# A softmax over long rows: the last six chunks' stores issued by SyncE behind the last load instead of by ScalarE

## The chip, the cores and the metric

The kernel runs on one core of a Trainium2 chip. The metric is the device time of one execution in microseconds (us), the median of several runs. The core's compute engines used here are VectorE (DVE) and ScalarE (ACT); SyncE (SP) computes nothing and issues transfers. Transfers between the device memory and the core's on-chip memory are carried out by 16 DMA engines; an instruction on SP or ACT only starts one. All transfers started by SP stand in one queue, in the profile q1, all those started by ACT in another, q10.

## What is computed

A softmax over the last axis of a tensor of 16 x 256 rows with 32768 float32 elements each, with a temperature of 1.0:

```python
def setup_inputs():
    batch, seq, vocab = 16, 256, 32768
    return {
        "logits": np.random.randn(batch, seq, vocab).astype(np.float32),
        "temperature": 1.0,
    }

def reference(logits, temperature):
    scaled = logits / temperature
    scaled = scaled - scaled.max(axis=-1, keepdims=True)
    exp_scaled = np.exp(scaled)
    return (exp_scaled / exp_scaled.sum(axis=-1, keepdims=True)).astype(np.float32)
```

The input is 537 MB and the output as much. Each is moved once.

## The kernel before

**Tiling.** Each row of 32768 elements is cut into two halves of 16384, which lie in two neighbouring partitions. So 64 rows fill the 128 partitions and form a group `g`; there are `G` = 64 groups. A group is worked on in `C` = 2 chunks of `_CW` = 8192 columns: 128 partitions x 8192 float32, which is 32 KB in each partition and 4.19 MB in all. The chunks are numbered `i` = 0 to 127 over the whole run (`n_chunks` = 128); group 63 has chunks 126 and 127.

**Buffers.** Six chunk buffers (`_BUFS` = 6) lie side by side in the tensor `X`; chunk `i` uses buffer `i % 6`. A chunk is loaded into its buffer, changed in place, and stored from it. So load `i + 6` can be issued only when store `i` has landed.

**One group** (`compute`, called once for each group). For each chunk DVE takes the negated maximum of its 8192 columns (line 156, output `t`), and ACT takes the exponential in place with that maximum as bias, and sums it up on the way (line 170). When both chunks are done, DVE swaps the values of neighbouring partitions (line 183), so that both halves of a row know each other's maximum and sum; the common maximum (line 187), the correction factors of the chunks (line 194, on ACT, output `ee`), the row's sum (line 200) and its reciprocal (line 212) follow. All of these are tiny. Then DVE scales each chunk in place by its factor and the reciprocal (line 221). Only after that can a chunk be stored.

**Edges.** In the last group (`g == G - 1`) the step is `_EDGE` = 4096 columns and no longer 8192: chunks 126 and 127 are loaded, reduced, scaled and stored in two halves of 2.10 MB each. The first group is loaded in halves as well.

**Order by hand.** Each engine's instructions are executed in the order in which the program issues them; the order between engines is made by semaphores. A `Stream` (`sp`, `dve`, `act`) stands for an engine: its `wait` makes that engine wait for given semaphore values, and its `done` counts an instruction of that engine. A `Landing` counts a buffer's transfers that have arrived. `load(i)` (lines 103 to 118) is issued by SP, with a wait for the store that used the buffer before (line 106), and the transfer itself on line 112. `store(i)` (lines 120 to 133) is issued by ACT, with a wait for DVE's scaling of the piece (line 126, `scaled[i, s]`), and the transfer on line 128. The main loop (lines 232 to 241) first issues six loads, and then for each group: `compute(g)`, and for each of its chunks `store(i)` and `load(i + 6)`, as long as there is such a chunk. So the last load, that of chunk 127, is issued in the round of chunk 121, and no load stands behind it in the program. At the end SP waits for all stores (line 242; the wait itself is on line 31, in `Stream.wait`).

Of the kernel before, what the change touches and what calls it, by code (L numbers as in the profile page):

```python
# [8 lines left out]
_CW = 8192  # L9
_BUFS = 6  # L10
_EDGE = 4096


class Stream:
# [41 lines left out]
def kernel(  # L56
# [6 lines left out]
    nc = tc.nc  # L63
# [15 lines left out]
    n_chunks = G * C  # L79
# [10 lines left out]
    sp = Stream(nc, nc.sync, "sp")  # L90
    dve = Stream(nc, nc.vector, "dve")
    act = Stream(nc, nc.scalar, "act")
    loads = [[Landing(nc, f"ld{b}{h}") for h in range(_CW // _EDGE)] for b in range(_BUFS)]
    stores = [Landing(nc, f"st{b}") for b in range(_BUFS)]
    scaled = {}
# [4 lines left out]
    def spans(total, step):  # L100
        return [(s, min(step, total - s)) for s in range(0, total, step)]
# [18 lines left out]
    def store(i):  # L120

        g, c = divmod(i, C)
        b = i % _BUFS
        rows = slice(g * P, (g + 1) * P)
        for s, n in spans(_CW, _EDGE if g == G - 1 else _CW):
            act.wait(scaled[i, s])
            stores[b].add(
                nc.scalar.dma_start(
                    out=o[rows, c * _CW + s : c * _CW + s + n],
                    in_=X[:, b * _CW + s : b * _CW + s + n],  # L130
                )
            )
        freed[b] = [stores[b].token()]
# [100 lines left out]
    for g in range(G):  # L234
        compute(g)
        for c in range(C):
            i = g * C + c
            store(i)
            j = i + _BUFS
            if j < n_chunks:  # L240
                load(j)
# [36 lines left out]
```

## Time and profile before

| What | Value |
|---|---|
| Time, median of 3 runs | 2497.72 us (2497.65 to 2498.47) |
| Time of the profiled execution | 2497.72 us |
| Its span, first to last instruction | 2495.9 us |
| DVE busy | 1723.7 us, 69% of the span |
| ACT busy | 944.5 us, 38% of the span |
| Moved | 1073.84 MB, mean 430 GB/s |
| q1 (loads, issued by SP) | 536.88 MB, 49.9% of the 16 DMA engines' span |
| q10 (stores, issued by ACT) | 536.88 MB, 49.8% of the 16 DMA engines' span |
| Load of a whole chunk, issue to landing | 26.6 us (median) |
| Store of a whole chunk, issue to landing | 49.4 us (median) |
| Maximum of a whole chunk, DVE line 156 | 8.69 us |
| Exponential of a whole chunk, ACT line 170 | 7.12 us |

The page gives busy times by engine, the span in 40 slices, the queues, the chain of work that ended last, the costliest groups of instructions, and the transfers. Such a page is read beside closer views of the same trace: the chain in order of time, the instructions in order of time, who waited for whom, and the engines' busy time and the transfers' rate in chosen stretches. Times in these views are in us from the start of the span. The DMA share in a short stretch can come out slightly over 1.

"SPq" and "ACTq" are the sequencers of SP and ACT, in which transfers are issued; "L112" is line 112.

### The profile page before, as it was taken

What the parts mean: (1) busy time and instruction counts of PE and PEld (TensorE: products, weight loads), DVE (VectorE), ACT (ScalarE), POOL (GpSimd) and SP (SyncE); (2) the same over time, 40 slices, a digit from 0 to 9 for tenths busy, and PEclk for the clock granted to TensorE, in tenths of its full rate; (3) what the DMA queues carried; (4) which work ended last, traced back from release to release, by engine and by line L of the source; (5) the groups of instructions that cost most, each with busy time, mean ns of one, the idle gap of its engine ahead of it and who ended that gap; (6) DMA issues with size and microseconds to landing.
All of it is one profiled execution on the core that took longest, in us unless ns stands there. A gap on an engine that the chain in (4) does not pass through costs nothing.

```text
span 2495.9 us, 1288 instructions
## 1 busy us (share of the span) xinstructions
DVE 1723.7 (69%) x644; ACT 944.5 (38%) x325; POOL 0.2 (0%) x4
## 2 busy tenths in 40 slices
DVE  6777766767667676676766767767667676676763
ACT  3344334343343433434334333343333433434332
POOL 0000000000000000000000000000000000000000
DMA  9999999999999999999999999999999999999997
GB/s 412 432 433 435 430 436 430 436 430 436 432 434 435 431 435 430 436 431 434 435 431 436 429 437 430 436 432 433 435 430 435 431 436 432 434 434 431 435 433 337
DMA packets 37738, 1073.84 MB, mean 430 GB/s; under 512 B 4192, under 2 KB 4192, under 8 KB 4192
## 3 DMA queue, kind: packets, MB, share of 16 engines
q1 hardware_dynamic: 19008, 536.88, 49.9%
q10 hardware_dynamic: 18720, 536.88, 49.8%
q14 instruction: 10, 0.08, 0.0%
HBM read 536.87 MB, written 536.87 MB: 430 GB/s over the span
## 4 chain that ended last, share of the span: by engine, by line
DMA 62%; another core or an unknown queue 15%; DVE 15%; ACT 7%; SPq 0%; issue 0%; DVEq 0%
DMA out_dram<-xs 38%; DMA xs<-in_logits_dram 23%; DVE t L156 9%; ACT xs L170 7%; DVE xs L221 5%; SPq L112 0%; ACT ee L194 0%; DVE row L212 0%; DVE row L187 0%; DVE t L183 0%; DVE junk L200 0%; DVE row L200 0%; SPq L273 0%; DVEq L31 0%
## 5 line engine op out<-in xcount | busy, mean ns | idle before, releaser
L170 ACT ACTIVATE xs<-xs,t 128x8192 f32<-128x8192 f32 (+1 forms) x130 | 912.1, 7016 | 1498.5 <-DVE t L156 1498.5
L156 DVE TENSOR_REDUCE t<-xs 128x1 f32<-128x8192 f32 (+1 forms) x130 | 1111.1, 8551 | 263.8 <-DMA xs<-in_logits_dram 263.8
L221 DVE TENSOR_SCALAR xs<-xs,ee,row 128x8192 f32<-128x8192 f32 (+1 forms) x130 | 576.6, 4478 | 2.3
L183 DVE LOAD_MASK_SELECT t<-t x64 | 0.9, 14 | 463.1 <-ACT xs L170 463.1
L194 ACT ACTIVATE ee<-t,row 128x4 f32<-128x4 f32 x64 | 19.0, 297 | 27.0 <-DVE row L187 27.0
L200 DVE CUSTOM_DVE_ANT_1 junk<-ee,t 128x4 f32<-128x4 f32 x64 | 10.4, 163 | 23.3 <-ACT ee L194 23.3
L170 ACT ACTIVATION_READ_ACCUMULATOR xs<-xs,t 128x1 f32 x130 | 24.2, 186 | 0.0
L212 DVE RECIPROCAL row<-row 128x1 f32<-128x1 f32 x64 | 10.5, 164 | 2.2
L187 DVE TENSOR_REDUCE row<-t 128x1 f32<-128x4 f32 x64 | 10.1, 157 | 2.2
L183 DVE STREAM_SHUFFLE t<-t 128x4 f32<-128x4 f32 x64 | 9.9, 155 | 0.0
L200 DVE DVE_READ_ACCUMULATOR2_ANT row<- 128x1 f32 x64 | 5.3, 82 | 0.0
L170 ACT ACT_TABLE_LOAD x1 | 1.3, 1283 | 0.9 <-SPq L82 0.9
L259 POOL MEMSET const-bfloat16-1.0<- 128x1 bf16 x1 | 0.1, 101 | 0.0
L259 POOL MEMSET const-uint8-127<- 128x1 uint8 x1 | 0.1, 101 | 0.0
L259 POOL MEMSET const-float32-0.0<- 128x1 f32 x1 | 0.1, 98 | 0.2 <-issue 0.2
L259 POOL MEMSET const-float32-1.0<- 128x1 f32 x1 | 0.1, 98 | 0.0
## 6 DMA issues: line engine op xcount, KB each, us to landing
out_dram<-xs ACTq DMA_DIRECT2D x126, 4096.0 KB, 49.4
xs<-in_logits_dram SPq DMA_DIRECT2D x124, 4096.0 KB, 26.6
xs<-in_logits_dram SPq DMA_DIRECT2D x8, 2048.0 KB, 21.2
out_dram<-xs ACTq DMA_DIRECT2D x4, 2048.0 KB, 10.2
```

Of the source, the lines that this page charges most:

```text
L156: nc.vector.tensor_reduce(out=t[:, k : k + 1], in_=xs, axis=mybir.AxisListType.X, op=A.max, negate=True)
L170: nc.scalar.activation(out=xs, in_=xs, func=Exp, bias=t[:, k : k + 1], scale=inv_t, accum_out=t[:, K + k : K + k + 1],)
L183: nc.vector.stream_shuffle(out=t[:, 2 * K : 4 * K], in_=t[:, 0 : 2 * K], mask=swap)
L187: nc.vector.tensor_reduce(out=r[:, 0:1], in_=tv[:, :, 0, :], axis=mybir.AxisListType.XY, op=A.min)
L194: nc.scalar.activation(out=ev, in_=tv[:, :, 0, :], func=Exp, bias=r[:, 0:1], scale=-1.0)
L200: nc.vector.tensor_tensor_reduce(out=j_[:, 0 : 2 * K].rearrange("p (a k) -> p a k", a=2), in0=ev, in1=tv[:, :, 1, :], scale=1.0, scalar=0. ...
L212: rc = dve.done(nc.vector.reciprocal(out=r[:, 2:3], in_=r[:, 1:2]))
L221: nc.vector.tensor_scalar(out=xs, in0=xs, scalar1=e[:, k : k + 1], scalar2=r[:, 2:3], op0=A.mult, op1=A.mult,)
L259: nc = _bacc.Bacc("TRN2", target_bir_lowering=False, num_devices=1)
```

## The change

A constant `_LATE` = 6 is added. For the last six chunks, 122 to 127 (those of groups 61, 62 and 63), the wait for the scaling and the issue of the store go to SP; for all chunks before, they stay with ACT. Sizes, pieces, semaphores and buffers are the same, and so are all loads and the arithmetic.

```diff
 _BUFS = 6
 _EDGE = 4096
+_LATE = 6
...
         rows = slice(g * P, (g + 1) * P)
+        q = sp if i >= n_chunks - _LATE else act
         for s, n in spans(_CW, _EDGE if g == G - 1 else _CW):
-            act.wait(scaled[i, s])
+            q.wait(scaled[i, s])
             stores[b].add(
-                nc.scalar.dma_start(
+                q.engine.dma_start(
                     out=o[rows, c * _CW + s : c * _CW + s + n],
                     in_=X[:, b * _CW + s : b * _CW + s + n],
                 )
             )
```

In program order, the eight issues of these stores (four of a whole chunk, four of half a chunk) stand on SP behind the load of chunk 127 and ahead of the last wait.

## The prediction

> **What bounds the kernel now.** I read the profile in this order: the page's slices, its chain, the same chain near the end, the engines there, and the transfers stretch by stretch. First the slices, and the share of the span by engine in the chain that ended last:
>
> ```profile
> DMA  9999999999999999999999999999999999999997
> GB/s 412 432 433 435 430 436 430 436 430 436 432 434 435 431 435 430 436 431 434 435 431 436 429 437 430 436 432 433 435 430 435 431 436 432 434 434 431 435 433 337
> ...
> DMA 62%; another core or an unknown queue 15%; DVE 15%; ACT 7%; SPq 0%; issue 0%; DVEq 0%
> ```
>
> The transfer engines are full in every slice but the last, at about 433 GB/s, loads and stores together. The kernel must move 1073.8 MB and the rate doesn't change, so time can be won only where the transfers stand idle: at the start, and in the last slice, which moves 337. The table by stretch (columns: us, busy time of DVE, ACT and POOL, clock, DMA share, GB/s) shows where in that slice:
>
> ```profile
> 5.00:45.00 40.00, 22.85 (x10) 14.72 (x5) 0.00 (x0) 1.00 1.01 433
> ...
> 2442.00:2458.00 16.00, 4.42 (x1) 3.80 (x2) 0.00 (x0) 1.00 1.00 431
> 2458.00:2463.00 5.00, 1.14 (x1) 0.00 (x0) 0.00 (x0) 1.00 0.95 410
> 2463.00:2464.00 1.00, 1.00 (x1) 0.00 (x0) 0.00 (x0) 1.00 0.23 98
> 2464.00:2466.00 2.00, 2.00 (x1) 0.00 (x0) 0.00 (x0) 1.00 0.08 33
> 2466.00:2467.50 1.50, 0.28 (x1) 1.19 (x1) 0.00 (x0) 1.00 0.05 22
> 2467.50:2469.00 1.50, 0.00 (x0) 1.50 (x1) 0.00 (x0) 1.00 0.00 0
> 2469.00:2474.50 5.50, 3.88 (x8) 1.41 (x3) 0.00 (x0) 1.00 0.00 0
> 2474.50:2475.50 1.00, 1.00 (x1) 0.00 (x0) 0.00 (x0) 1.00 1.23 524
> ```
>
> The first row is loads alone: 433 GB/s. At the end the share falls to a quarter at 2463, to 0.05 (less than one of the 16 transfer engines) after 2466, and is nothing from 2467.5 to 2474.5. The packet records say it more exactly: 13 transfer engines end their work near 2463.1, two at 2465.2 and 2465.7, one at 2467.54; the next packet begins at 2474.57. The slowest transfer engine is thus idle for **7.03 us**, and every stretch before that it is busy. Why it is idle, the chain in order of time says:
>
> ```profile
> 2412.33 0.33 SPq L112
> 2412.65 0.04 issue
> 2412.70 49.14 DMA xs<-in_logits_dram
> 2461.83 0.02 issue
> 2461.86 4.43 DVE t L156
> ```
>
> The last half of chunk 127's load is issued at 2412.70 and takes 49.14 us, because stores 122 to 125 run beside it. Its maximum, exponential, row factors and scaling follow with no transfer left to cover them, and the last four stores (line 128) are issued from 2473.73 on.
>
> **The change, part by part.** I number chunks as the code does. *What ACT loses*: eight store issues (chunks 122 to 125 whole, 126 and 127 in halves) of 0.338 us each at line 128, 2.7 us, and the waits on line 126. ACT idles there for 18.1 us at a time for DVE's maxima, so this is worth nothing; without that idle time it would gain 2.7 us of ACT.
>
> *What SP gets*: the same eight waits and issues, behind load 127, its last. Issues on SP took 0.328 us (line 112), 0.926 us in the longest case, so 2.6 to 7.4 us in all; I take 0.33 each, since the first store stands free. Behind them on SP are only the later stores and the end's wait (line 242); no load can be held up. Nobody waits for these eight stores but that last wait, as no load reuses their buffers.
>
> *What is held back*: store 122 is ready at 2386.3 and is issued then, yet lands 40.6 us later, at 2426.9: it stands on ACT's queue behind stores 120 and 121. Store 121 was issued at 2352.0 and lands 60.3 us later, at 2412.3, which is also what releases load 127. So until 2412.3 nothing changes. From there ACT's queue is empty and SP's holds the rest of load 126, load 127, then the stores.
>
> *The loads*: the first half of 126 gets the transfer engines from 2403.3 (load 125 lands: issue 2376.6 plus 26.6) to 2417.8 (2396.0 plus 21.8): 2.10 MB in 14.5 us, 144 GB/s, a third of 433. At 2412.3, 62% of it is there; 0.8 MB and three halves of 2.1 MB are left, 7.1 MB. Alone at 433 GB/s (the 5 to 45 row) they take 16.4 us and land by **2428.7** in place of 2461.8. The other end of this price is the present 144 GB/s beside stores, with which they would land where they do now; I take the first, as nothing runs beside them.
>
> *The arithmetic*, from these two rows of the order in time:
>
> ```profile
> 2420.38 9.00 DVE L221 TENSOR_SCALAR xs<-xs,ee,row 128x8192 f32<-128x8192 f32 x2
> 2429.30 8.74 DVE L156 TENSOR_REDUCE t<-xs 128x1 f32<-128x4096 f32 x2
> ```
>
> DVE is free at 2429.4 and then has all four halves: 4 x 4.37 = 17.5 us, to 2446.9 (ACT's 3.9 us for each keeps up). From the end of the last maximum (2461.86 + 4.43 = 2466.29) to the first store's issue (2473.73) is 7.44 us today, so that store is issued at 2454.3 and the fourth 7.0 us later, at 2461.3.
>
> *The stores*: 122 to 125 are 16.8 MB, 38.8 us at 433 GB/s: 2428.7 + 38.8 = 2467.5, the moment at which they end today, as it must be with the same bytes. By then the last group's stores have long been issued: with 0.84 us from issue to first packet (2473.73 to 2474.57) the first needs to go by 2466.7, and goes 12.4 us earlier. For the transfer engines that end at 2463.1 the margin is 8 us. So the last stores follow without a gap. Today they take from 2474.57 to the last landing, 2480.7 + 14.0 = 2494.7; all of it moves ahead by 7.03.
>
> *Unknown*: no row shows a store behind a load on one queue. Below, the turn costs nothing, as between loads on SP's queue; above, one pause of 0.84 us to start plus 0.34 us for a landing (last packet 2494.40, landed 2494.74), 1.2 us. I take nothing: that is how two transfers follow each other there. Unknown too is whether the lag of the slowest transfer engine stays. Today the gap lets it catch up; if the others could take it over, another 2467.5 - 2463.1 = 4.4 us would be won, and this is the lower bound. I take it as staying: its 32 KB packets take 1.213 us with the others idle and with them busy.
>
> **Sum**: span 2495.9 - 7.0 = 2488.9. This execution took 2497.72 us, 1.8 more than its span, and is the median of the three runs (2497.65 to 2498.47). Forecast 2497.72 - 7.03 = **2490.7 us**, 0.28% less.
>
> [...]
>
> **Rivals.** *The last stores come late*: if the loads of 126 and 127 land more than 12 us after 2428.7, the gap stays in part. For it: their rate today. Against: ACT's queue is empty then. Half of the gap left: 2494.2; all of it: 2497.7. The same 2497.7 holds if SP's stores somehow don't stand behind load 127, but the loop issues it after store 121 and before store 122.
>
> *One queue pauses between transfers* (the slower side): two queues can cover each other's starts, one can't. From 2412.3 SP's queue has eleven transfers to come after the half in progress: three load halves, four whole stores, four half stores. A pause of 1.2 us at each is 13.2 us, less 7.0: 2503.9. It decides from six pauses on. Against: the eight loads at the start stood on that one queue alone, and by issue and time to landing came at 8.3, 13.2, 18.0, 23.0, 32.7 and 42.4 us, 4.9 for a half and 9.7 for a whole chunk, which is 433 GB/s without a pause. For: those are loads behind loads only. A pause at the turn alone gives 2491.9.
>
> *The lag is won too*: 2490.7 - 4.4 = 2486.3. Against: the 22 GB/s of the last transfer engine at 2466, which didn't quicken.
>
> **How the numbers follow.** Forecast 0.80, own range 2489.8 to 2492.0. Lag won 0.05. Late stores or no effect 0.09. Pauses 0.06. Below 2492.7 (0.2%, or 5.0 us, is about what a measurement tells from no change) lie the first two, 0.85; within 0.2%, 0.09; slower, 0.06. The range 2488.0 to 2493.5 holds the forecast, the pause at the turn, and the near parts of the lag and of late stores.
>
> **What would show it.** In the profile after: load 127 lands at about 2428.7, 16 us after its issue and not 49; the stretch 2412 to 2428 has only loads, at 433 GB/s; the maxima of the last group follow each other from 2429.4 with no wait for a load; the last four stores are issued between 2454 and 2462 and the last takes some 26 us to land, not 14; no stretch of zero transfers; the chain ends in stores. I am wrong if the share drops at 2428 or between stores, if the last four are issued later than 2466, or if the stores' rate on SP's queue is below 420 GB/s.

## The result and the profile after

The changed kernel takes **2490.88 us** (median of 8 runs, 2490.03 to 2491.78) against 2497.68 us for the kernel before (8 runs, 2497.07 to 2498.69). The ratio is 0.9972, with a 95% interval of 0.9961 to 0.9983. The profiled execution took 2490.77 us, with a span of 2489.0 us, 6.9 us less than before.

First the page of the kernel after: its slices, and its two transfer queues (packets, MB, share of the 16 DMA engines' span).

```profile
DMA  9999999999999999999999999999999999999999
GB/s 412 430 437 430 436 432 432 436 430 437 430 435 433 431 436 431 436 431 434 433 431 437 430 436 432 432 435 430 437 431 434 433 431 437 430 436 432 432 426 393
...
q1 hardware_dynamic: 20160, 562.05, 52.4%
q10 hardware_dynamic: 17568, 511.71, 47.6%
```

The last slice is full where it was 7 tenths full, and moves 393 GB/s where it moved 337. The last slice but one has 426 against 433; in the slices before, the two lines differ by up to 6 GB/s in both directions. The 25 MB of six chunks' stores have moved from q10 to q1. The stretches at the end, with the same columns as before (us, busy time of DVE, ACT and POOL, clock, DMA share, GB/s):

```profile
2458.00:2463.00 5.00, 3.01 (x2) 0.00 (x0) 0.00 (x0) 1.00 0.97 419
2463.00:2464.00 1.00, 0.00 (x0) 0.00 (x0) 0.00 (x0) 1.00 0.81 344
2464.00:2466.00 2.00, 0.00 (x0) 0.00 (x0) 0.00 (x0) 1.00 1.07 459
...
2469.00:2474.50 5.50, 0.00 (x0) 0.00 (x0) 0.00 (x0) 1.00 1.01 432
2474.50:2482.00 7.50, 0.00 (x0) 0.00 (x0) 0.00 (x0) 1.00 1.01 435
2482.00:2484.00 2.00, 0.00 (x0) 0.00 (x0) 0.00 (x0) 1.00 0.48 205
2484.00:2486.00 2.00, 0.00 (x0) 0.00 (x0) 0.00 (x0) 1.00 0.15 66
2486.00:2487.50 1.50, 0.00 (x0) 0.00 (x0) 0.00 (x0) 1.00 0.05 22
```

Where the kernel before moved nothing for 7 us, this one moves 432 GB/s. DVE has nothing to do any more by 2463: its work lies beside the stores. The slow fall at the end, which stood at 2463 to 2467.5 before, is now the very end: twelve of the 16 transfer engines are done near 2483, the other four follow, the last at 2487.5.

The chain in order of time and the instructions show how the arithmetic moved (start, us, what):

```profile
2403.21 8.70 DVE t L158
...
2420.31 9.00 DVE xs L223 x2
2429.31 17.32 DVE t L158 x4
2446.63 0.02 issue
2446.65 3.81 ACT xs L172 x2
...
2451.63 9.38 DVE xs L223 x4
```

The four maxima of the last group follow the scaling of the group before at once, 17.32 us together. Before, the last two of them waited 8.87 and 10.54 us for their loads. The second half of chunk 127's load is issued at 2412.6 and lands 17.0 us later, not 49.1. The last four stores are issued at 2454.1 to 2461.0 and the last of them lands 26.8 us later, at 2487.8, where the kernel before had 2494.7.

### The profile page after: what moved, and what is told of

It is laid out like the page before. It is cut to its first block, busy times and chain, and to the rows that moved or that the text cites. A ratio compares the mean times of both kernels' runs of the same rounds, so it can differ in the third digit from the quotient of the medians.

```text
span 2489.0 us, 1288 instructions
## 1 busy us (share of the span) xinstructions
DVE 1723.5 (69%) x644; ACT 944.5 (38%) x325; POOL 0.2 (0%) x4
## 4 chain that ended last, share of the span: by engine, by line
DMA 58%; DVE 18%; another core or an unknown queue 15%; ACT 8%; SPq 0%; issue 0%; DVEq 0%
DMA out_dram<-xs 37%; DMA xs<-in_logits_dram 21%; DVE t L158 11%; ACT xs L172 7%; DVE xs L223 6%; ACT ee L196 0%; SPq L113 0%; DVE row L214 0%; DVE row L189 0%; DVE t L185 0%; DVE junk L202 0%; DVE row L202 0%; SPq L275 0%; DVEq L32 0%
## 6 DMA issues: line engine op xcount, KB each, us to landing
out_dram<-xs ACTq DMA_DIRECT2D x122, 4096.0 KB, 49.7
```

## The experiments

Each is compared with the kernel before, run on the same chip beside it; those of one set share these runs. The diffs are against the kernel after.

### How many stores go behind the loads

**Four, three or two chunks in place of six** (runs late4, late3, late2):

```diff
-_LATE = 6
+_LATE = 4
```

> Only chunks 124 to 127 are stored by SP; 122 and 123 stay with ACT. Theory (the gain is the idle time of the slowest transfer engine between store 125's end and the last four stores): loads 126 and 127 keep a third of 433 GB/s until store 123 lands at 2441.4, have 2.9 MB left then, and land at 2441.4 + 6.7 = 2448.1, before 2467.5 - 0.84 - 7.44 - 4.43 = 2454.8. No gap is left: 2490.9 us, as with six. Rival (the gain comes from the stores moved, a share for each): two thirds of 6.8 us, 2493.2 us.

Measured: 2490.7 us (2490.15 to 2490.95), ratio 0.9971 (0.9959 to 0.9982). As with six: two stores fewer behind the loads cost nothing. The packet records of this run have no gap.

> Only chunks 125 to 127 are stored by SP. Theory: load 127 keeps a third of 433 GB/s until store 124 lands at 2456.4, has 0.7 MB left then and lands at 2458.1; the first of the last stores is issued at 2458.1 + 4.43 + 7.44 = 2470.0 and moves its first byte at 2470.8, 2.9 us after the slowest transfer engine ran dry at 2467.9. So 4.1 of 7.0 us are won: 2493.6 us. Rival (a share for each store moved): half of 6.8 us, 2494.3 us, with no gap in sight or the whole gap.

Measured: 2494.66 us (2493.96 to 2495.0), ratio 0.9987 (0.9978 to 0.9996). Its stretches at the end:

```profile
2463.00:2464.00 1.00, 0.55 (x1) 0.41 (x1) 0.00 (x0) 1.00 0.15 66
2464.00:2468.50 4.50, 0.63 (x6) 3.69 (x3) 0.00 (x0) 1.00 0.08 36
2468.50:2471.80 3.30, 3.26 (x3) 0.00 (x0) 0.00 (x0) 1.00 0.00 0
2471.80:2474.50 2.70, 2.70 (x2) 0.00 (x0) 0.00 (x0) 1.00 1.15 485
```

The gap is there in part: from the last packet of store 125 (2468.46) to the next packet (2471.84) it is 3.4 us, against 7.03 before. The time itself is nearer to the rival's 2494.3 than to the 2493.6 worked out; it is the part of a gap, which the rival doesn't have, that tells the two apart. Of the miss of 1.1 us, 0.3 is in the working: it counts its 2.9 us from the landing of store 125 (2467.87) and not from its last packet (2467.54). The rest lies ahead of the gap: load 127 lands at 2459.1, 1.0 us later than worked out, and store 125 0.9 us later than before. Why was not taken apart; in late2, whose stores 122 to 125 run beside the loads as before, its last packet comes just as late.

> Only chunks 126 and 127 are stored by SP. Theory: the stores 122 to 125 run beside the last loads as before, load 127 lands at 2461.8, and the whole gap of 7 us stays: 2497.7 us. Rival (a share for each store moved): a third of 6.8 us, 2495.4 us. A third theory, that the last four stores go faster from SP's queue than from ACT's, says less than 2497 us as well.

Measured: 2498.31 us (2497.5 to 2498.88), ratio 1.0001 (0.9992 to 1.0009): no change. The gap is 7.03 us as before (packets end at 2468.46, the next begins at 2475.49), and the last four stores take 6.3 to 14.0 us to land, as before. So SP's queue is not the faster one for them, and the gain is no share for each store moved: with 2, 3, 4 and 6 chunks it is nothing, 3.2, 7.1 and 6.8 us. It goes by how much of the gap is closed.

### The same order without SP

**All stores by ACT, but 122 to 125 held back until load 127 has landed** (run held_act). ACT issues them between the exponentials of groups 62 and 63:

```diff
-        q = sp if i >= n_chunks - _LATE else act
+        q = act
+        if n_chunks - _LATE <= i < n_chunks - 2:
+            act.wait(*landed[n_chunks - 1])
...
-            store(i)
+            if i < n_chunks - _LATE:
+                store(i)
...
+        if g == G - 2:
+            for i in range(n_chunks - _LATE, n_chunks - 2):
+                store(i)
+        if g == G - 1:
+            for i in range(n_chunks - 2, n_chunks):
+                store(i)
```

> All stores stay with ACT; those of chunks 122 to 125 are issued by ACT between the exponentials of groups 62 and 63, each after a wait for load 127's landing. Theory (what counts is that the last loads go first, so that the last group's arithmetic lies beside stores; by which engine they are issued counts for nothing): loads land at 2429, the stores follow after a pause of 0.84 to 2.3 us, the last ones without a gap: 2491.5 to 2493 us. Rival (the gain is SP's queue itself, or ACT relieved of eight issues): 2497.7 us as before, or more, since ACT now waits.

Measured: 2492.3 us (2491.81 to 2493.34), ratio 0.9978 (0.9968 to 0.9987). Four fifths of the gain, 5.5 of 6.8 us, come without a single store on SP; it is the order that counts. What is missing is a pause, which the stretches of this run show:

```profile
2412.00:2424.00 12.00, 4.39 (x7) 7.40 (x3) 0.00 (x0) 1.00 0.99 423
2424.00:2428.70 4.70, 4.70 (x2) 0.00 (x0) 0.00 (x0) 1.00 0.11 45
2428.70:2430.00 1.30, 1.30 (x2) 0.00 (x0) 0.00 (x0) 1.00 0.95 403
```

From 2424.0 to 2428.7 most transfer engines have no work while the last ones finish the loads; only after the landing at 2428.7 do the stores start. Store 122 lands 11.9 us after load 127, where 9.7 us is the time of a chunk: the pause costs the slowest transfer engine 2.2 us. Queued behind the loads on one queue, the stores start without it, but there the turn from loads to stores costs 0.8 us, as the section on the prediction shows. The difference, 1.4 us, is that of the two times, 2492.3 and 2490.9.

### How much arithmetic the stores cover

**Two or four idle maxima on DVE in the last group** (runs extra2 and extra4; the result isn't used):

```diff
+_EXTRA = 2
...
+    Z = nc.alloc_sbuf_tensor("extra", [P, 8], fp32)
...
         dve.wait(sums[-1])
+        if g == G - 1:
+            for k in range(_EXTRA):
+                dve.done(
+                    nc.vector.tensor_reduce(
+                        out=Z[:, k : k + 1], in_=xs, axis=mybir.AxisListType.X, op=A.max, negate=True
+                    )
+                )
```

> The kernel after with two more maxima of 4096 columns on DVE in the last group, behind its last exponential (their result is not used): 8.7 us more between the last load and the last four stores. Theory: the first of these stores is issued at 2454.1 + 8.7 = 2462.8 and has its first packet at 2463.6, before the slowest transfer engine runs dry at 2468.0: nothing is lost, 2490.9 us. Rival (the arithmetic of the last group still stands on the path to the end): 2490.9 + 8.7 = 2499.6 us.

Measured: 2490.62 us (2490.36 to 2491.15), ratio 0.9971 (0.9959 to 0.9982). The added work is there, in the instructions of this run in order of time, and costs nothing:

```profile
2450.81 8.74 DVE L190 TENSOR_REDUCE extra<-xs 128x1 f32<-128x4096 f32 x2 [3.87 <-ACT xs L175]
```

> The same with four more maxima, 17.4 us. Theory: the first of the last stores is issued at 2471.5, first packet at 2472.3, 4.3 us after the slowest transfer engine runs dry at 2468.0: a gap opens again, 2490.9 + 4.3 to 4.7 = 2495.4 us. Rival (arithmetic on the path): 2490.9 + 17.4 = 2508.3 us. A theory in which the cover is as wide as the whole of the stores 122 to 125: 2490.9 us.

Measured: 2495.45 us (2495.22 to 2495.86), ratio 0.999 (0.9981 to 0.9999). The stretches of this run:

```profile
2463.00:2464.00 1.00, 1.00 (x2) 0.00 (x0) 0.00 (x0) 1.00 0.23 98
2464.00:2467.70 3.70, 3.70 (x3) 0.00 (x0) 0.00 (x0) 1.00 0.08 35
2467.70:2472.00 4.30, 3.83 (x8) 0.30 (x1) 0.00 (x0) 1.00 0.00 0
2472.00:2474.50 2.50, 2.50 (x2) 0.00 (x0) 0.00 (x0) 1.00 0.99 419
```

17.4 us of added work cost 4.6 us, and the gap accounts for it: by the packet records it is 4.5 us (2467.55 to 2472.07). So the room in the kernel after is between 8.7 and 17.4 us, and by this cost 17.4 - 4.6 = 12.8 us.

### Two more stores on SP

**Eight chunks** (run late8). Now the stores of 120 and 121, for whose landing loads 126 and 127 wait, stand on SP's queue among these loads:

```diff
-_LATE = 6
+_LATE = 8
```

> Chunks 120 to 127 are stored by SP, so that the stores of 120 and 121 stand on SP's queue between its last loads, and loads 126 and 127 are issued only when they have landed. Theory: nothing is queued elsewhere by then, and the transfer engines pause twice for a landing and a start, 0.34 + 0.84 us each: 2490.9 + 2.4 = 2493.3 us, with two short dips of the DMA share near 2400 and 2420. Rival (more stores on SP's queue is better, a share for each): 2490.9 - 2.3 = 2488.6 us. Rival (one queue pauses between all its transfers): far more than 2.4 us.

Measured: 2499.96 us (2499.37 to 2500.26), ratio 1.0008 (0.9999 to 1.0016). The two further stores throw away the whole gain; the 2.1 us above the kernel before are not clear of noise. The theory had the sign and missed the size: 9.1 us over the kernel after, not 2.4. The stretches of this run show two kinds of loss:

```profile
2385.00:2391.00 6.00, 6.00 (x3) 0.00 (x0) 0.00 (x0) 1.00 0.95 300
2391.00:2399.00 8.00, 8.00 (x1) 0.00 (x0) 0.00 (x0) 1.00 1.00 430
2399.00:2402.00 3.00, 3.00 (x2) 2.47 (x1) 0.00 (x0) 1.00 0.05 22
2402.00:2403.50 1.50, 1.50 (x1) 1.50 (x1) 0.00 (x0) 1.00 0.20 44
2403.50:2407.00 3.50, 3.50 (x1) 3.24 (x2) 0.00 (x0) 1.00 0.93 360
2407.00:2411.00 4.00, 1.09 (x1) 2.88 (x1) 0.00 (x0) 1.00 1.06 455
2411.00:2415.50 4.50, 0.12 (x2) 4.33 (x2) 0.00 (x0) 1.00 1.07 350
...
2434.00:2439.00 5.00, 4.47 (x2) 4.30 (x3) 0.00 (x0) 1.00 1.04 328
```

One is the pause, as awaited but longer: near 2402 (and again at 2425) nothing is queued until a store has landed. From that landing to the landing of the next half chunk it takes 7.1 us where 4.9 is its time, so 2.25 us for each pause. The other shows at 2385 and 2411, and again at 2434: the transfer engines count as busy, share 0.95 to 1.07, and move only 300 to 350 GB/s. Each time the last load before a store is in transfer: load 125 takes 12.2 us from the landing before it in place of 9.7, the second halves of 126 and 127 take 6.25 and 6.4 us in place of 4.9. That is 2.5, 1.35 and 1.5 us. Two pauses and three such turns are 9.85 us; less the 0.8 us that one turn costs in the kernel after, this comes to the 9.1 us. The terms are read from this one trace; no run changed them one at a time.

### Which transfer engines lag, and why

**Sixteen tiny loads behind the last store** (run probe, executed once), on 1, 2, 3 and up to 16 partitions:

```diff
...
+    for k in range(16):
+        probes[k].add(
+            nc.sync.dma_start(
+                out=Z[0 : k + 1, 64 * k : 64 * k + 64], in_=x[0 : k + 1, 64 * k : 64 * k + 64]
+            )
+        )
-    sp.wait(*[s.token() for s in stores])
+    sp.wait(*[s.token() for s in stores], *[s.token() for s in probes])
```

> The kernel after with sixteen tiny loads on SP's queue behind its last store, the first of 1 partition, the next of 2, and so on to 16 (256 bytes in each partition). If partitions of such a load go to transfer engines in a fixed order, the landing times step up where the first lagging transfer engine is included: a step of about 2 us or more shows which of the 16 lag. If the lag of 4.5 us at the end is not tied to fixed transfer engines, all land alike, near 2488. Time: 2491 to 2493 us.

Measured: 2494.02 us in the one run, 1 us over the range expected. The load on one partition lands at 2484.1, on two at 2487.4, on three at 2487.6, on four at 2488.8, and each further one about 0.18 us later. In the single counts of the load on sixteen partitions, 13 come by 2486.8 and three at 2489.7, 2489.9 and 2491.0; in that on five, already three come after 2487. So, if each further partition adds one transfer engine, as the steps suggest but no run shows by itself, the lag sits on three of the transfer engines that the first five partitions use, by the steps the second, fourth and fifth, and on none of the other eleven.

**More instruction fetches** (run fill): 2560 tiny instructions on GpSimd, which nobody waits for.

```diff
+_FILL = 2560
...
+    Z = nc.alloc_sbuf_tensor("fill", [P, _FILL], fp32)
+    for k in range(_FILL):
+        nc.gpsimd.memset(Z[:, k : k + 1], 0.0)
```

> The kernel after with 2560 tiny GpSimd instructions (one column set to zero each) at the start, which nobody waits for. The trace before has 10 instruction fetches of 8 KB in the run, and at each of them the landings show one transfer engine fall some 0.6 to 1 us further behind. Theory (the fetches make the lag that the end waits for): about 20 more fetches, 0.95 us each, on one transfer engine: it lies 19 us behind instead of 4.4, and the run ends some 14 us later, 2505 us; less if they fall on several transfer engines or lag where the transfers have slack. Rival (a fetch costs its own 0.31 us of packet time alone): 6.2 us on one transfer engine, 1.8 us beyond the present lag, 2492.7 us. Rival (fetches don't matter): 2490.9 us.

Measured: seven of the 10 runs took 2500.26 to 2535.33 us, median 2500.46; the other three took 2555.75 to 2569.34 and are left out of the ratio, 1.0035 (1.0001 to 1.007). The kernel before took 2497.92 us beside it, on another chip than in the runs above. The page has 30 packets in the instruction queue where the kernel after has 10, and the last stretches of the profiled execution (2500.46 us) show one transfer engine alone for nearly 7 us:

```profile
q14 instruction: 30, 0.25, 0.0%
```

```profile
2480.00:2489.00 9.00, 0.00 (x0) 0.00 (x0) 0.00 (x0) 1.00 1.00 430
2489.00:2490.50 1.50, 0.00 (x0) 0.00 (x0) 0.00 (x0) 1.00 0.51 218
2490.50:2497.30 6.80, 0.00 (x0) 0.00 (x0) 0.00 (x0) 1.00 0.06 24
```

In the landing records the last of the 16 counts of each load falls behind by 0.65 us at each of the first fetches (0.99, 1.65, 2.29 and 2.96 us at 8.7, 14.2, 19.8 and 25.3 us). When all twenty are through, a load lands 16.2 us later than in the kernel after, 0.8 us for each of the twenty if all of it is theirs; the last count then stays 11.6 us behind the first for most of the run. At the end 9.6 us of this are left. The forecast of 14 us was too large, but both rivals fall: here a fetch cost more than its packet's 0.31 us, and it added up.

The fills also share the first 120 us with DVE's work, but that isn't what holds back the one transfer engine: through load 5, which lands at 47 us, the other 15 counts come within 0.15 us of the kernel after and the last alone is late, by 5.2 us. From there on one scaling on DVE takes 12.66 us in place of 4.54, the stores after it are issued some 11 us later, and the other transfer engines too end up 5 to 6 us late; how much of that comes from DVE and how much from waiting for the slowest one was not taken apart. Why some runs took up to 2569 us is open.

## Why the prediction was right

Forecast 2490.7 us, measured 2490.88. Point by point:

- **The bound and the gap.** Right, and shown by late2, late3 and extra4: the time follows the length of the stretch in which nothing moves. Gaps of 7.0, 3.4 and 4.5 us go with 2498.3, 2494.7 and 2495.5 us, no gap with 2490.6 to 2490.9 (late4, extra2 and the kernel after). Closing 7.03 us won 6.9 us of span.
- **What is held back costs nothing.** Right: nothing changes until store 121 lands, at 2412.25 here and at 2412.31 before. ACT's eight issues were worth nothing, as costed: in held_act ACT keeps them all, and the pause less the turn accounts for what that run lacks.
- **The loads alone.** Forecast to land at 2428.7, landed at 2429.6. The step that was off is the price of the *turn from loads to stores on one queue*. The prediction's bounds were nothing and 1.2 us, and it took nothing. It is 0.8 us: the last half of load 127 takes 5.7 us where the halves before take 4.9. In held_act, where the same loads have no store behind them on their queue, it takes 4.9, and none of their packets is slowed. So one of the prediction's signs, loads alone at 433 GB/s from 2412 to 2428, did not come true: it is 411. The stretches of the kernel after show where:

```profile
2412.00:2422.50 10.50, 2.84 (x7) 7.45 (x3) 0.00 (x0) 1.00 1.00 429
2422.50:2424.50 2.00, 2.00 (x1) 0.00 (x0) 0.00 (x0) 1.00 1.03 270
2424.50:2428.00 3.50, 3.50 (x2) 0.00 (x0) 0.00 (x0) 1.00 1.02 435
2428.00:2463.00 35.00, 28.66 (x15) 15.51 (x9) 0.00 (x0) 1.00 1.00 433
```

- **The arithmetic and its room.** Maxima to 2446.6 (2446.9 forecast), first store of the last four issued at 2454.1 (2454.3), last at 2461.0 (2461.3). The room of 12.4 us is 12.8 by extra4. The sign that the chain ends in stores can't be read from the view: it lists the scaling last, before and after alike, though 8.7 us of added arithmetic cost nothing in extra2.
- **The last stores.** They were moved ahead as a whole, from 2494.7 to 2487.8, as worked out (2487.7). That this is closer than the terms before it is luck: the 0.8 us of the turn, which the sum left out, came back behind it. Store 125 lands at 2468.35, only 0.5 us later than before. From there to the last landing (2487.8) it is 19.4 us, while before it was 20.2 us from the first packet (2474.57) to the last landing, which held the 0.34 us of a landing and some slower packets at the start.
- **The lag stays.** Right: at the end the share falls as it did at 2463 before, and the last landing's counts spread over 4.7 us, as those of store 125 did before.
- **The rate.** Right but for the turn: 433 GB/s from 2428 to 2463, with stores alone but for the first 1.6 us, and 429 from 2412 to 2422.5, with loads alone.
- **The rivals.** Late stores: late3 and extra4 show them at work, but not here. The pauses of one queue: between the transfers of SP's queue the kernel after has none but the turn; a pause came where, with nothing else queued, a transfer was issued only after another had landed, as late8 and held_act show, and it was 2.2 us and not 1.2.

Of the versions without added work, four and six late chunks are the best, at 2490.7 and 2490.9 us; the runs don't tell them apart.

## What to carry to other kernels

In a kernel that is bound by transfers, look for the stretch in which nothing moves, and ask which transfers that are ready could have been kept for it: here stores that nobody waited for stood beside the last loads and took two thirds of the rate from them (the first half of load 126 got 144 of 433 GB/s, an estimate from its landing 14.5 us after load 125's). Hold such stores back until the last load is through, by as many as cover the arithmetic that follows, and no store on whose landing a load still depends. Here a queue that was filled ahead did this without a pause, but for the 0.8 us of the turn; a wait for a landing ahead of the next issue, with nothing else queued, cost 2.2 us each time (held_act and late8).

## What the runs showed of the hardware

- **The turns from loads to stores cost 0.8 to 2.5 us, though the transfer engines looked busy.** In the kernel after, the DMA share is 1.03 at 270 GB/s from 2422.5 to 2424.5, and load packets at the turn take up to some three times as long (2.0 us in place of 0.61 for 16 KB): 0.8 us in all. In late8 the turns cost 1.35 to 2.5 us. In held_act, with no store queued behind the loads, no load packet of the last group takes more than 0.63 us. It was seen with two queues as well: in the kernel before, loads had run alone until the first store was issued on ACT's queue at 44.75 us. From 46.2 us on their 32 KB packets take 1.3 to 2.0 us in place of 1.21, and the rate falls from 437 to 385 GB/s for 4 us; the first packet of a store stands in the record at 49.7.

```profile
40.00:46.00 6.00, 5.96 (x3) 0.00 (x0) 0.00 (x0) 1.00 1.02 437
46.00:50.00 4.00, 4.00 (x2) 0.00 (x0) 0.00 (x0) 1.00 1.11 385
```

  What slows these packets was not tested.
- **At instruction fetches single transfer engines fell 0.3 to 1.0 us behind, and the lags added up.** In the kernel after, the last landing count falls 0.8 to 1.0 us further behind at five of the ten fetches (near 158, 641, 1145, 1650 and 2151 us) and ends 4.4 us behind the middle of the counts; the other five go with lags of some 0.3 to 0.7 us of other counts. In fill, after twenty fetches within 120 us, one transfer engine is 16.2 us later than in the kernel after. Between fetches the last count won little back: in the kernel after it goes from 1.05 us behind the middle at 173 us to 0.89 at 638. A gap made it good: in the kernel before, the counts of a store spread over 4.7 us ahead of the gap and over 0.2 behind it. The last store of the kernel after has its 16 counts from 2483.05 to 2487.79, and with the last it has landed: twelve transfer engines are done near 2483, and the end waits for the other four, whose last packet ends at 2487.5. A version that evens this out was not tried.
